# Rounded two-part products for three sums of squares, and one stretch for the scan's small transposes and products

## The chip, the cores and the metric

The kernel runs on one core of one Trainium2 chip. The core has a matrix engine (TensorE, PE in the profile, with its weight loads as PEld), three engines for element work (VectorE or DVE, ScalarE or ACT, GpSimd or POOL) and queues that start transfers (SP's, GpSimd's and ScalarE's). The metric is device time in microseconds (us) of one launch.

## What is computed

The reference is one layer of a streaming encoder for two request groups, 256 prompt positions and 32 sample positions, 288 in all, in float32. Cut to what matters here:

```python
def rmsnorm(x, g):
    y = x * lax.rsqrt(jnp.mean(x * x, axis=-1, keepdims=True) + EPS)
    return y * g

def ssd_scan(xh, dt, A, Bm, Cm, D, h0):          # 32 heads in 2 groups, chunks of 64
    acum = jnp.cumsum(dt * A, axis=-1)            # per chunk
    lmat = jnp.exp(jnp.where(causal, acum[..., :, None] - acum[..., None, :], -jnp.inf))
    cb = jnp.einsum('bclgn,bcsgn->bcgls', Cc, Bc)
    y_diag = jnp.einsum('bcgls,bcgjls,bcsgjp->bclgjp', cb, lmat, xc)
    decay_states = jnp.exp(acum[..., -1:] - acum)
    ...
    return y_diag + y_off + D[..., None] * xh, h_last

def run_layer(x, ...):
    proj = rmsnorm(x, norm_mix_pre) @ w_in        # u, z, xBC, dt
    y_pool = pool_mixer(u, ...)
    y_ssd = ssd_mixer(z, xbc, dt_raw, ...)        # conv, silu, ssd_scan, gate, rmsnorm per group of 1024
    x = x + rmsnorm(concat([y_pool, y_ssd]) @ w_out, norm_mix_post)
    x = x + rmsnorm(ConvFFN(rmsnorm(x, norm_ffn_pre)), norm_ffn_post)
```

## The kernel before

Activations lie with channels on the 128 partitions and the 288 positions along the free axis. Every large product is made of three: weights and activations are each split into a rounded high part and a low part in the format fp32r (`split_w`, L124 to L138; `split_from`, L101), and `mm3` (L141 to L144) adds high times high, high times low and low times high into one accumulator. ScalarE rounds the weights (L136), VectorE subtracts to get the low part (L137), and each pair of tiles comes from a ring of four buffers. `project` (L146) streams the weights from memory through this for 256 output channels at a time.

The stages follow each other: the first stage (`prepare`, the loop over CHUNKS, L324 to L358) multiplies the first 768 columns of w_in while the input arrives, and its order on every engine is written out by hand (`pin`, which puts an instruction behind the one traced before it on its engine). Then come the projections for the scan's channels (xs) and the gates (z), among which eight `ssd_quad` calls do the scan for four heads each; then u and the pooling, w_out, the states, the feed-forward block, and a pinned end. Outside the pinned parts a planner sets the order on each engine from its own estimate of when things are ready and from the order in which the code traced them.

Three places matter.

The sums of squares. A sum over channels is a matmul of a 128x128 tile of float32 ones with a float32 tile of squares, which leaves the sum on every partition. The first is L349, in the next to last chunk of the first stage, behind 24 of its products: ScalarE and VectorE gather the squares in `sq2` (L315 to L318), VectorE adds its two halves (L339), TensorE sums, ScalarE takes the square root (L352), VectorE the reciprocal (L353), and all results of the first stage are scaled by it. `rstd_all` (L659 to L670) does the same for the scan's two groups of 1024 channels (`rg0` in the middle of the z projections, `rg1` after the first u projection; their squares are gathered by GpSimd in `gsum`, L684) and, pinned, for the feed-forward block (`r2`, over `xsum`).

The scan's tables. dt and the running sums g of 32 heads are computed on 32 partitions (L472 to L505). From g come the decay rows `dec` (three exponentials on ScalarE, L510, and one product with dt on VectorE, L511). `ssd_quad` wants them by position, so nine transposes of 32 rows by 128 columns (L518 to L520: g, dt and dec in each of three blocks of positions) go through three PSUM tiles, and VectorE copies each out in two pieces, `tok` and `tokd` (L521, L522).

The head columns and C.B. One 32-row matmul (L530) spreads the skip factor D and the last decay of each head into `dcol`; six matmuls of 128 rows (L546 to L548) make the products of C and B for the two groups, from which VectorE makes the masked table `cbt` (L549 to L552).

Of the kernel before, what the change touches and what calls it, by code (L numbers as in the profile page):

```python
# [16 lines left out]
P = 128  # L17
# [39 lines left out]
def body(  # L57
# [34 lines left out]
    def aux(shape, name):  # L92
        return aux_ps.tile(shape, F32, tag="aux", name=name)
# [230 lines left out]
    for i, (kb, n) in enumerate(CHUNKS):  # L324
# [13 lines left out]
        if i == len(CHUNKS) - 2:  # L338
            pin(dve.tensor_tensor(sq2[:, :NT], sq2[:, :NT], sq2[:, NT:], op=ALU.add))  # L339
        w = ahead_w.pop(0)  # L340
        products = [
# [4 lines left out]
        for q, (r, m, k, x) in enumerate(products):  # L346
            if i == len(CHUNKS) - 2 and q == 24:
                p_ = aux([P, NT], "prs")
                pin(pe.matmul(p_, ones, sq2[:, :NT], start=True, stop=True))  # L349
                rstd = const.tile([P, NT], F32, tag="spread", bufs=3, name="rstd")  # L350
                last_split[:] = [
                    pin(act.activation(rstd, p_, AF.Sqrt, bias=eps_t, scale=1.0 / D_MODEL)),  # L352
                    pin(dve.reciprocal(rstd, rstd)),  # L353
                ]
# [17 lines left out]
    act.activation(g_ssd, col["ssd_norm"], AF.Copy, scale=0.5)  # L372
    sel = const.tile([HEADS, 2], F32, name="sel")
    pick = const.tile([HEADS, NX], F32, name="pick")
    sel64 = const.tile([HEADS, 2, 64], F32, name="sel64")
    with tc.issue_after(last_split[1].ins):
        dve.tensor_reduce(sel, id32.rearrange("h (t r) -> h r t", r=2), axis=AX.X, op=ALU.add)
        dve.tensor_reduce(pick, id32.rearrange("h (t r) -> h t r", r=2), axis=AX.X, op=ALU.add)
        dve.tensor_copy(sel64, sel.unsqueeze(2).broadcast_to([HEADS, 2, 64]))

    start.close()


    mixer = ExitStack()
    mp = mixer.enter_context(tc.tile_pool(name="mixer", bufs=1))
    sc_stage = const.tile([P, 2, 3, NXC], F32, name="sc_stage")
    np_stage = const.tile([P, 2, 15, NU], F32, name="np_stage")
# [107 lines left out]
    dve.tensor_tensor_scan(r, scan_one, adt, 0.0, op0=ALU.mult, op1=ALU.add)  # L495
    g = mp.tile([HEADS, 4, MW], F32, tag="m", bufs=2, name="g")[:, 0, :]
    t0, t1, t2 = r[:, 63:64], r[:, 127:128], r[:, 191:192]
# [9 lines left out]
    sp.dma_start(out=g_d, in_=g)  # L507
    dec = htile("dec", tag="gsum")
    for (o, n), go, last in zip(BLK, (0, 256, 384), (255, 383, 415)):
        act.activation(dec[:, o : o + n], g[:, go : go + n], AF.Exp, bias=g[:, last : last + 1], scale=-1.0)  # L510
    dve.tensor_tensor(dec, dec, dt, op=ALU.mult)  # L511


    tok = mp.tile([P, 3, 2, HEADS], F32, name="tok")
    tokd = const.tile([P, 3, HEADS], F32, name="tokd")
    for b, (o, go) in enumerate(((0, 0), (P, 256), (TAIL, MW - P))):
        p_ = aux([P, 3, HEADS], "ptok")
        pe.transpose(p_[:, 0, :], g[:, go : go + P], id32)  # L518
        pe.transpose(p_[:, 1, :], dt[:, o : o + P], id32)
        pe.transpose(p_[:, 2, :], dec[:, o : o + P], id32)  # L520
        dve.tensor_copy(tok[:, b, :, :], p_[:, 0:2, :])  # L521
        dve.tensor_copy(tokd[:, b, :], p_[:, 2, :])  # L522

# [4 lines left out]
    dve.tensor_scalar(hv[:, NX:], pick, elast, None, op0=ALU.mult)  # L528
    p_ = aux([P, 2 * NX], "phv")
    pe.matmul(p_, sel64.rearrange("h r q -> h (r q)"), hv, start=True, stop=True)  # L530
    dcol = const.tile([P, 2 * NX], F32, name="dcol")
# [11 lines left out]
    for gi in range(2):  # L543
        blocks_out(b_d, gi, bc[gi], mp, 2)
        p_ = aux([P, MW], "pcb")
        pe.matmul(p_[:, 0:256], bc[gi][:, 0:P], bc[2 + gi][:, 0:NP_], start=True, stop=True)  # L546
        pe.matmul(p_[:, 256:384], bc[gi][:, P:NP_], bc[2 + gi][:, P:NP_], start=True, stop=True)
        pe.matmul(p_[:, 384:], bc[gi][:, TAIL:], bc[2 + gi][:, NP_:], start=True, stop=True)  # L548
        dve.tensor_tensor(cbt[:, gi, 0:128], p_[:, 0:128], tri, op=ALU.mult)  # L549
# [108 lines left out]

    def rstd_all(sq, scale, name, pin=False):  # L659

        p_ = aux([P, NT], "psum_t")
        ins = pe.matmul(p_, ones, sq, start=True, stop=True)
        if pin:
            tc.keep_in_program_order(ins)
            sums_at.append(ins)
        with tc.high_priority(offset=800 if pin else 0):
            o = const.tile([P, NT], F32, tag="spread", bufs=3, name=name)
            act.activation(o, p_, AF.Sqrt, bias=eps_t, scale=scale)
            dve.reciprocal(o, o)
        return o  # L670
# [69 lines left out]
    for i in range(NX // 2):  # L740
# [7 lines left out]
        if i == 5:  # L748
            rg.append(rstd_all(gsum[0], 0.25 / 1024, "rg0"))
        run_quads(Z_RATE[i])  # L750
# [19 lines left out]
    ups = [project(win, [(512, 256)], xn, K16)]  # L770
    rg.append(rstd_all(gsum[1], 0.25 / 1024, "rg1"))
    mixer.close()
# [276 lines left out]
    def up(tiles, spare=()):  # L1049
# [5 lines left out]
        def out(m, p_):  # L1055
            waiting.append((each[m], p_))
            if not norm_2 and m == SUMS_AFTER:
                norm_2.append(rstd_all(xsum, 1.0 / D_MODEL, "r2", pin=True))
            while norm_2 and waiting:
# [279 lines left out]
```

## Time and profile before

| | before |
|---|---|
| timed runs, median of 3 | 1336.0 us (1335.72 to 1336.15) |
| profiled execution, first to last instruction (its span) | 1333.3 us |
| granted TensorE clock, mean | 1.000 |
| TensorE busy | 1325.7 us, 99% of the span |
| VectorE, ScalarE, GpSimd busy | 885.5, 665.1, 241.7 us |
| bytes moved by DMA | 249.52 MB |

A profile is one execution, taken by the hardware. Times are from the start of the span. The rows name the line of the kernel, the engine, and out<-in by the program's names. A busy time of a group of matmuls counts overlapping ones once; a single matmul's length includes its way through the array, so the distance from one start to the next, not the length, is what it adds. The chain of waits follows the work that ended last back from the end, and its pieces give that distance; a piece in it stands some 0.07 to 0.17 us later than the start of the same instruction in the timeline. Releasers ("<-") are inferred from semaphores.

### The profile page before, as it was taken

To read this page: it belongs to the slowest core of one execution; us is meant where nothing else is said; L and a number is where in the kernel's file an instruction comes from. 1 tells how busy PE (TensorE), PEld (TensorE's weight loads), DVE (VectorE), ACT (ScalarE), POOL (GpSimd) and SP (SyncE) were. 2 spreads that over 40 slices of the span, in tenths; PEclk is the share of its full clock that TensorE was granted. 3 is DMA by queue.
4 is the path that set the end of the run, shared out by engine and by line. 5 is a ranking of instruction groups with operands and counts; after the bars stand their busy time and mean duration, and the time that the engine had idled before them with its cause. 6 is when DMAs were issued, how large, how long until landed. Compare 5 with 4: busy or idle time off the path is not lost.

```text
span 1333.3 us, 25388 instructions
## 1 busy us (share of the span) xinstructions
PE 1325.7 (99%) x10127; PEld 1314.2 (99%) x10127; DVE 885.5 (66%) x1501; ACT 665.1 (50%) x995; POOL 241.7 (18%) x386
## 2 busy tenths in 40 slices
PE   9999999999999999999999999999999999999998
PEld 9999999999999999999999999999999999999997
DVE  7999987879544488976766643335666666754454
ACT  7557767446443456544444433334454444444442
POOL 2343231222122310211211200001121111201110
PEclk9999999999999999999999999999999999999999
DMA  8678884455555446766554454454554555466753
GB/s 329 192 216 266 272 252 156 155 199 210 190 191 202 143 145 227 210 184 181 167 177 158 153 172 156 160 182 162 179 165 159 167 170 170 159 227 188 206 177 111
DMA packets 110230, 249.52 MB, mean 187 GB/s; under 512 B 64480, under 2 KB 75840, under 8 KB 87584
## 3 DMA queue, kind: packets, MB, share of 16 engines
q1 hardware_dynamic: 105920, 233.61, 54.6%
q0 software_dynamic: 3808, 13.77, 2.9%
q8 instruction: 79, 1.29, 0.4%
q10 hardware_dynamic: 384, 0.52, 0.1%
q14 instruction: 39, 0.32, 0.1%
HBM read 235.91 MB, written 11.95 MB: 186 GB/s over the span
## 4 chain that ended last, share of the span: by engine, by line
PE 98%; DVE 0%; DMA 0%; ACT 0%; SPq 0%; issue 0%
PE acc L142 30%; PE acc L144 30%; PE acc L143 30%; PE acc L355 2%; PE acc_x L355 1%; PE py L613 1%; PE acc L1200 0%; PE acc L1201 0%; DMA xg<-in_x_g 0%; PE acc_t L1223 0%; PE pst L938 0%; PE acc_x L143 0%; PE acc_x L142 0%; PE acc_x L144 0%; PE pst L905 0%; PE py L615 0%
## 5 line engine op out<-in xcount | busy, mean ns | idle before, releaser
L137 DVE TENSOR_TENSOR wlo<-raw,whi 128x1024 fp32r<-128x1024 f32 (+1 forms) x396 | 472.0, 1193 | 346.1 <-ACT whi L136 344.8
L136 ACT ACTIVATE whi<-raw 128x1024 fp32r<-128x1024 f32 (+1 forms) x396 | 408.5, 1033 | 503.2 <-PE acc L143 420.4
L142 PE MATMUL acc<-hn,whi 128*128 128x288 f32 x1376 | 404.3, 296 | 0.0
L143 PE MATMUL acc<-hn,whi 128*128 128x288 f32 x1376 | 403.8, 294 | 0.2 <-DVE hn L994 0.2
L144 PE MATMUL acc<-hn,wlo 128*128 128x288 f32 x1376 | 403.3, 294 | 0.0
L143 PEld LDWEIGHTS acc<-hn,whi 128*128 128x128 f32 x1376 | 259.9, 189 | 0.7 <-DVE hn L994 0.7
L144 PEld LDWEIGHTS acc<-hn,wlo 128*128 128x128 f32 x1376 | 259.9, 189 | 0.0
L142 PEld LDWEIGHTS acc<-hn,whi 128*128 128x128 f32 x1376 | 257.3, 187 | 0.1
L142 PE MATMUL acc<-fa,whi 128*128 128x288 f32 x660 | 195.5, 296 | 0.0
L143 PE MATMUL acc<-fa,whi 128*128 128x288 f32 x660 | 195.4, 296 | 0.0
L144 PE MATMUL acc<-fa,wlo 128*128 128x288 f32 x660 | 195.1, 296 | 0.0
L142 PE MATMUL acc<-xn,whi 128*128 128x288 f32 x608 | 180.8, 297 | 0.0
L143 PE MATMUL acc<-xn,whi 128*128 128x288 f32 x608 | 179.1, 295 | 0.0
L144 PE MATMUL acc<-xn,wlo 128*128 128x288 f32 x608 | 178.8, 294 | 0.0
L143 PEld LDWEIGHTS acc<-fa,whi 128*128 128x128 f32 x660 | 124.5, 189 | 0.0
L142 PEld LDWEIGHTS acc<-fa,whi 128*128 128x128 f32 x660 | 124.1, 188 | 0.0
L144 PEld LDWEIGHTS acc<-fa,wlo 128*128 128x128 f32 x660 | 123.8, 188 | 0.0
L1027 POOL COPY fc_stage<-ebuf 128x4 f32<-128x4 f32 x88 | 25.7, 293 | 503.5 <-DVE ebuf L1026 460.1
L143 PEld LDWEIGHTS acc<-xn,whi 128*128 128x128 f32 x608 | 114.9, 189 | 0.1
L144 PEld LDWEIGHTS acc<-xn,wlo 128*128 128x128 f32 x608 | 114.8, 189 | 0.0
L142 PEld LDWEIGHTS acc<-xn,whi 128*128 128x128 f32 x608 | 114.0, 187 | 0.8 <-issue 0.5
L1033 DVE SCALAR_TENSOR_TENSOR fc<-ebuf,cols,fc 128x290 f32<-128x290 f32 x176 | 90.4, 517 | 2.9 <-ACT fc L1031 0.3
(333 smaller groups left out, 1766.5 us busy)
## 6 DMA issues: line engine op xcount, KB each, us to landing
raw<-in_w_up SPq DMA_DIRECT2D x80, 1024.0 KB, 5.1
raw<-in_w_in SPq DMA_DIRECT2D x38, 1024.0 KB, 5.4
raw<-in_w_down SPq DMA_DIRECT2D x32, 1024.0 KB, 5.0
raw<-in_w_out SPq DMA_DIRECT2D x24, 1024.0 KB, 5.0
raw<-in_w_down SPq DMA_DIRECT2D x16, 768.0 KB, 4.2
raw<-in_w_up SPq DMA_DIRECT2D x14, 512.0 KB, 3.9
gb<-g_d POOLq DMA_DIRECT2D x8, 832.0 KB, 7.1
raw<-in_w_first SPq DMA_DIRECT2D x5, 768.0 KB, 13.0
```

Of the source, the lines that this page charges most:

```text
L136: act.activation(hi, raw[:, k : k + n, :], AF.Copy)
L137: dve.tensor_tensor(lo, raw[:, k : k + n, :], hi.bitcast(F32), op=ALU.subtract)
L142: then(pe.matmul(out, wh, a[:, 0, :], start=start, stop=False))
L143: then(pe.matmul(out, wh, a[:, 1, :], start=False, stop=False))
L144: then(pe.matmul(out, wl, a[:, 0, :], start=False, stop=stop))
L355: pin(pe.matmul(first[m], w[:, k, r * NB + m * P :][:, :P], xn[kb + k][:, x, :], start=kb + k + r + x == 0, stop=kb + k == KD - 1 and r == ...
L613: ins = pe.matmul(y[c, 0:256], xw[:, 0, f_], m[:, h, 0:256], start=True, stop=False)
L1027: pool.tensor_copy(fc_stage[:, :, :, i], e[:, 256:324].rearrange("p (s c) -> p s c", c=34)[:, :, 0:2])
L1033: dve.scalar_tensor_tensor(c, e[:, r_ : r_ + 290], f_w[:, r_, i : i + 1], c, op0=ALU.mult, op1=ALU.add)
```

## The change

The first sum: VectorE makes a rounded copy of the gathered squares and the rest by subtraction, and TensorE adds two fp32r products with a tile of ones that is in fp32r already (`busy`). `rstd_all` does likewise where it isn't pinned, with the rounded copy on ScalarE and a new tile of rounded ones, `ones_r`; the two parts are taken from the mixer's ring "sq" of two buffers. The pinned sum stays.

g, a copy of dt and the decay rows are put on partitions 0 to 31, 32 to 63 and 64 to 95 of one tile, `turned`; the decay product becomes three, one behind each exponential, and two copies bring dt over. Three transposes of 96 rows replace nine, into one PSUM tile that the head columns share, and two copies replace six. `follow` leaves the first of these transposes to the planner and pins each of the rest, the head columns' matmul and the six C.B matmuls behind the one before. `sel`, `pick` and `sel64` move from the constants to the mixer's pool, and `dec` from the ring "gsum" to the ring "z", with 416 columns.

```diff
@@ -337,6 +337,9 @@
             ))
         if i == len(CHUNKS) - 2:
             pin(dve.tensor_tensor(sq2[:, :NT], sq2[:, :NT], sq2[:, NT:], op=ALU.add))
+            sq_r = xin.tile([P, 2 * NT], F32R, tag="sq", bufs=1, name="sq_r")
+            pin(dve.tensor_copy(sq_r[:, :NT], sq2[:, :NT]))
+            pin(dve.tensor_tensor(sq_r[:, NT:], sq2[:, :NT], sq_r[:, :NT].bitcast(F32), op=ALU.subtract))
         w = ahead_w.pop(0)
         products = [
             (r, m, k, x) for m in (2, 3, 4, 5, 0, 1) for k in range(n) for r, x in ((0, 0), (0, 1), (1, 0))
@@ -346,7 +349,8 @@
         for q, (r, m, k, x) in enumerate(products):
             if i == len(CHUNKS) - 2 and q == 24:
                 p_ = aux([P, NT], "prs")
-                pin(pe.matmul(p_, ones, sq2[:, :NT], start=True, stop=True))
+                for c in (slice(0, NT), slice(NT, 2 * NT)):
+                    pin(pe.matmul(p_, busy[:, 0:P], sq_r[:, c], start=c.start == 0, stop=c.start > 0))
                 rstd = const.tile([P, NT], F32, tag="spread", bufs=3, name="rstd")
                 last_split[:] = [
                     pin(act.activation(rstd, p_, AF.Sqrt, bias=eps_t, scale=1.0 / D_MODEL)),
@@ -370,19 +374,20 @@
     act.activation(pah, cols[:, c0 : c0 + 5 * NXC], AF.Copy, scale=0.5)
     g_ssd = const.tile([P, NX], F32, name="g_ssd")
     act.activation(g_ssd, col["ssd_norm"], AF.Copy, scale=0.5)
-    sel = const.tile([HEADS, 2], F32, name="sel")
-    pick = const.tile([HEADS, NX], F32, name="pick")
-    sel64 = const.tile([HEADS, 2, 64], F32, name="sel64")
+    start.close()
+
+
+    mixer = ExitStack()
+    mp = mixer.enter_context(tc.tile_pool(name="mixer", bufs=1))
+    sel = mp.tile([HEADS, 2], F32, name="sel")
+    pick = mp.tile([HEADS, NX], F32, name="pick")
+    sel64 = mp.tile([HEADS, 2, 64], F32, name="sel64")
     with tc.issue_after(last_split[1].ins):
         dve.tensor_reduce(sel, id32.rearrange("h (t r) -> h r t", r=2), axis=AX.X, op=ALU.add)
         dve.tensor_reduce(pick, id32.rearrange("h (t r) -> h t r", r=2), axis=AX.X, op=ALU.add)
         dve.tensor_copy(sel64, sel.unsqueeze(2).broadcast_to([HEADS, 2, 64]))
-
-    start.close()
-
-
-    mixer = ExitStack()
-    mp = mixer.enter_context(tc.tile_pool(name="mixer", bufs=1))
+    ones_r = const.tile([P, P], F32R, name="ones_r")
+    act.activation(ones_r, ones, AF.Copy)
     sc_stage = const.tile([P, 2, 3, NXC], F32, name="sc_stage")
     np_stage = const.tile([P, 2, 15, NU], F32, name="np_stage")
     hist_c = col["hist_c"].rearrange("p (r t) -> p r t", t=NXC)
@@ -493,7 +498,8 @@
     dve.tensor_scalar(adt, dt, aneg, -1.0, op0=ALU.mult, op1=ALU.mult)
     r = htile("r", tag="z")
     dve.tensor_tensor_scan(r, scan_one, adt, 0.0, op0=ALU.mult, op1=ALU.add)
-    g = mp.tile([HEADS, 4, MW], F32, tag="m", bufs=2, name="g")[:, 0, :]
+    turned = mp.tile([P, 4, MW], F32, tag="m", bufs=2, name="g")[: 3 * HEADS, 0, :]
+    g, dt_rows, dec_rows = (turned[HEADS * i : HEADS * (i + 1), :] for i in range(3))
     t0, t1, t2 = r[:, 63:64], r[:, 127:128], r[:, 191:192]
     t12 = htile("t12", 1)
     dve.tensor_tensor(t12, t1, t2, op=ALU.add)
@@ -505,29 +511,34 @@
     dve.tensor_copy(g[:, 320:416], r[:, 192:288])
     g_d = dram.tile([HEADS, MW], F32, name="g_d")
     sp.dma_start(out=g_d, in_=g)
-    dec = htile("dec", tag="gsum")
+    dec = htile("dec", MW, tag="z")
     for (o, n), go, last in zip(BLK, (0, 256, 384), (255, 383, 415)):
-        act.activation(dec[:, o : o + n], g[:, go : go + n], AF.Exp, bias=g[:, last : last + 1], scale=-1.0)
-    dve.tensor_tensor(dec, dec, dt, op=ALU.mult)
-
+        act.activation(dec[:, go : go + n], g[:, go : go + n], AF.Exp, bias=g[:, last : last + 1], scale=-1.0)
+        dve.tensor_tensor(dec_rows[:, go : go + n], dec[:, go : go + n], dt[:, o : o + n], op=ALU.mult)
+    for o, n, go in ((0, P, 0), (P, NT - P, 256)):
+        dve.tensor_copy(dt_rows[:, go : go + n], dt[:, o : o + n])
+
+    small = []
+
+    def follow(ins):
+        return pin(ins) if small else small.append(ins)
 
     tok = mp.tile([P, 3, 2, HEADS], F32, name="tok")
     tokd = const.tile([P, 3, HEADS], F32, name="tokd")
-    for b, (o, go) in enumerate(((0, 0), (P, 256), (TAIL, MW - P))):
-        p_ = aux([P, 3, HEADS], "ptok")
-        pe.transpose(p_[:, 0, :], g[:, go : go + P], id32)
-        pe.transpose(p_[:, 1, :], dt[:, o : o + P], id32)
-        pe.transpose(p_[:, 2, :], dec[:, o : o + P], id32)
-        dve.tensor_copy(tok[:, b, :, :], p_[:, 0:2, :])
-        dve.tensor_copy(tokd[:, b, :], p_[:, 2, :])
+    p_t = aux([P, 9 * HEADS + 2 * NX], "ptok")
+    p_tok = p_t[:, : 9 * HEADS].rearrange("p (b h) -> p b h", b=3)
+    for b, go in enumerate((0, 256, MW - P)):
+        follow(pe.transpose(p_tok[:, b, :], turned[:, go : go + P], ident[: 3 * HEADS, : 3 * HEADS]))
 
     hv = htile("hv", 2 * NX)
     elast = htile("elast", 1)
     act.activation(elast, g[:, 415:416], AF.Exp)
     dve.tensor_scalar(hv[:, 0:NX], pick, hp[:, 2:3], None, op0=ALU.mult)
     dve.tensor_scalar(hv[:, NX:], pick, elast, None, op0=ALU.mult)
-    p_ = aux([P, 2 * NX], "phv")
-    pe.matmul(p_, sel64.rearrange("h r q -> h (r q)"), hv, start=True, stop=True)
+    p_ = p_t[:, 9 * HEADS :]
+    follow(pe.matmul(p_, sel64.rearrange("h r q -> h (r q)"), hv, start=True, stop=True))
+    dve.tensor_copy(tok, p_tok[:, :, : 2 * HEADS].rearrange("p b (r h) -> p b r h", r=2))
+    dve.tensor_copy(tokd, p_tok[:, :, 2 * HEADS :])
     dcol = const.tile([P, 2 * NX], F32, name="dcol")
     dve.tensor_copy(dcol, p_)
 
@@ -543,9 +554,9 @@
     for gi in range(2):
         blocks_out(b_d, gi, bc[gi], mp, 2)
         p_ = aux([P, MW], "pcb")
-        pe.matmul(p_[:, 0:256], bc[gi][:, 0:P], bc[2 + gi][:, 0:NP_], start=True, stop=True)
-        pe.matmul(p_[:, 256:384], bc[gi][:, P:NP_], bc[2 + gi][:, P:NP_], start=True, stop=True)
-        pe.matmul(p_[:, 384:], bc[gi][:, TAIL:], bc[2 + gi][:, NP_:], start=True, stop=True)
+        follow(pe.matmul(p_[:, 0:256], bc[gi][:, 0:P], bc[2 + gi][:, 0:NP_], start=True, stop=True))
+        follow(pe.matmul(p_[:, 256:384], bc[gi][:, P:NP_], bc[2 + gi][:, P:NP_], start=True, stop=True))
+        follow(pe.matmul(p_[:, 384:], bc[gi][:, TAIL:], bc[2 + gi][:, NP_:], start=True, stop=True))
         dve.tensor_tensor(cbt[:, gi, 0:128], p_[:, 0:128], tri, op=ALU.mult)
         dve.tensor_copy(cbt[:, gi, 128:256], p_[:, 128:256])
         dve.tensor_tensor(cbt[:, gi, 256:384], p_[:, 256:384], tri, op=ALU.mult)
@@ -656,13 +667,20 @@
                 tc.keep_in_program_order(ins)
         return p_
 
-    def rstd_all(sq, scale, name, pin=False):
+    def sq_parts(pool_):
+        return [pool_.tile([P, NT], F32R, tag="sq", bufs=2, name="sq_r") for _ in range(2)]
+
+    def rstd_all(sq, scale, name, sq_r, pin=False):
 
         p_ = aux([P, NT], "psum_t")
-        ins = pe.matmul(p_, ones, sq, start=True, stop=True)
         if pin:
-            tc.keep_in_program_order(ins)
+            ins = tc.keep_in_program_order(pe.matmul(p_, ones, sq, start=True, stop=True))
             sums_at.append(ins)
+        else:
+            act.activation(sq_r[0], sq, AF.Copy)
+            dve.tensor_tensor(sq_r[1], sq, sq_r[0].bitcast(F32), op=ALU.subtract)
+            for i in range(2):
+                pe.matmul(p_, ones_r, sq_r[i], start=i == 0, stop=i == 1)
         with tc.high_priority(offset=800 if pin else 0):
             o = const.tile([P, NT], F32, tag="spread", bufs=3, name=name)
             act.activation(o, p_, AF.Sqrt, bias=eps_t, scale=scale)
@@ -746,7 +764,7 @@
         if i == 0:
             xs_conv(NX // 2 - 1)
         if i == 5:
-            rg.append(rstd_all(gsum[0], 0.25 / 1024, "rg0"))
+            rg.append(rstd_all(gsum[0], 0.25 / 1024, "rg0", sq_parts(mp)))
         run_quads(Z_RATE[i])
         for j in range(2):
             gate_silu(2 * i + j)
@@ -768,7 +786,7 @@
 
 
     ups = [project(win, [(512, 256)], xn, K16)]
-    rg.append(rstd_all(gsum[1], 0.25 / 1024, "rg1"))
+    rg.append(rstd_all(gsum[1], 0.25 / 1024, "rg1", sq_parts(mp)))
     mixer.close()
     outp = ExitStack()
     op_ = outp.enter_context(tc.tile_pool(name="outp", bufs=1))
@@ -1055,7 +1073,7 @@
         def out(m, p_):
             waiting.append((each[m], p_))
             if not norm_2 and m == SUMS_AFTER:
-                norm_2.append(rstd_all(xsum, 1.0 / D_MODEL, "r2", pin=True))
+                norm_2.append(rstd_all(xsum, 1.0 / D_MODEL, "r2", None, pin=True))
             while norm_2 and waiting:
                 (kind, j), p_ = waiting.pop(0)
                 conv_[kind, j] = fconv(kind * NF + j, p_)
```

## The prediction

> **What bounds the kernel now.** I read first the head of the profile's page and the summary of the chain that ended last, then the list of waits, longest first.
>
> ```profile
> span 1333.3 us, 25388 instructions
> ...
> PE 1325.7 (99%) x10127; PEld 1314.2 (99%) x10127; DVE 885.5 (66%) x1501; ACT 665.1 (50%) x995; POOL 241.7 (18%) x386
> ...
> PE 98%; DVE 0%; DMA 0%; ACT 0%; SPq 0%; issue 0%
> ```
>
> ```profile
> ACT whi L136 <- PE acc L143: 420.4, 248, 2.8
> DVE wlo L137 <- ACT whi L136: 344.8, 225, 3.2
> ```
>
> TensorE is busy for 99% of the span and makes 98% of the chain. The two waits say the same from the other side: ScalarE, which rounds the weights, waits 420.4 us in all for buffers that TensorE must give back, and VectorE waits for ScalarE. Weights run ahead of the matmuls. So an edit is worth what it changes on TensorE's own queue: the time that its instructions hold the array, and any time for which that queue stands still. A microsecond on another engine counts only where a TensorE instruction then waits for it.
>
> The profiled execution's span is 1333.3 us and the median of the timed runs 1336.0, so 2.7 us lie around the span. The change touches nothing there; I sum against the span and add 2.7 at the end.
>
> **The three sums of squares.** The chain of waits, cut to short windows, gives what each instruction adds to TensorE's chain (start, time, what). The first sum, the group 0 sum and the group 1 sum, with neighbours:
>
> ```profile
> 37.90 0.93 PE acc L355 x7
> 38.84 0.48 PE prs L349 x2
> ```
>
> ```profile
> 242.00 0.49 PE psum_t L662 x2
> ```
>
> ```profile
> 284.61 0.13 PE acc L144
> 284.74 0.49 PE psum_t L662 x2
> 285.22 0.13 PE acc L142
> ```
>
> A float32 sum of 128x288 is one matmul in the code and two in the records (x2); the three hold TensorE for 0.48 + 0.49 + 0.49 = 1.46 us. A rounded product of the same 288 columns takes 0.93 / 7 = 0.133. Each sum becomes two of these: 3 x 2 x 0.133 = 0.80. That is **0.66 us less**, and since both prices stand side by side, the bounds are close to it (0.60 to 0.70). The pinned sum over xsum keeps its form and gives nothing.
>
> Each of the three now needs a rounded copy and a subtraction first. For groups 0 and 1 these are one operation on ScalarE and one on VectorE. What covers them, for group 1: the last addition into gsum, and the first use of the result.
>
> ```profile
> 276.69 1.42 POOL L684 TENSOR_TENSOR gsum<-gsum,sq 128x288 f32<-128x288 f32 x1 [1.49 <-ACT sq L683]
> ```
>
> ```profile
> L821 DVE TENSOR_TENSOR xs<-xs,rg x8: 444/450/452, 291.7 to 321.2; 128x288 f32<-128x288 f32 x8
> ...
> L669 DVE RECIPROCAL rg<-rg x2: 1952/1952/1952, 244.9 to 287.6; 128x288 f32<-128x288 f32 x2
> ```
>
> The sum's input is complete at 276.69 + 1.42 = 278.1, and TensorE takes the sum up at 284.7. Two operations of about 0.46 us (the VectorE row L339 below has that shape) fit into these 6.6 us: nothing on TensorE. If the planner moved the sum later by their 0.9 us, the result would be late by as much; the reciprocal now ends at 287.6 + 1.95 = 289.6, and its first use is at 291.7, so 2.1 us are left. Without the cover it would cost the 0.9. The two parts take both buffers of the ring from which the squares of the gates come, so ScalarE's next square waits for the sum; behind it on ScalarE stand roundings of weights, which have the 420.4 us of waiting to spare.
>
> The first sum has much less cover, and here the change adds a wait to a pinned queue. Its timeline on VectorE and GpSimd, and a row that shows how fast a released product starts:
>
> ```profile
> 37.47 0.46 DVE L339 TENSOR_TENSOR sq<-sq 128x288 f32<-128x288 f32 x1
> ```
>
> ```profile
> 44.73 0.20 POOL L408 COPY sc_stage<-ebuf 128x6 f32<-128x6 f32 x1 [12.78 <-DVE ebuf L402]
> ```
>
> ```profile
> 10.62 0.96 DVE L298 TENSOR_TENSOR w<-raw,w 128x768 fp32r<-128x768 f32 x1 [0.21 <-ACT w L294]
> ```
>
> ```profile
> 11.63 0.53 PE L355 MATMUL acc<-xn,w 128*128 128x288 f32 x2 [0.33 <-DVE w L298]
> ```
>
> The squares are added up by 37.47 + 0.46 = 37.93. For the rounded copy of 288 columns on VectorE the trace holds two neighbours that differ widely:
>
> ```profile
> L305 DVE CAST w<-raw 128x256 fp32r<-128x256 f32 x1 | 1.7, 1669 | 2.6 <-DMA raw<-in_w_first 2.6
> L483 DVE TENSOR_SCALAR ser<-s 32x288 f32<-32x288 f32 x1 | 0.3, 293 | 0.0
> ```
>
> ```profile
> 4.01 1.36 POOL L333 MEMSET ubuf<- 128x350 f32 x4
> ```
>
> The first is the same operation, 1.67 us from 3.86 on, and it ended at 5.53, soon after GpSimd had finished its fills at 4.01 + 1.36 = 5.37. The second is another operation with one input, 0.29 us. GpSimd is idle for the 12.78 us before 44.73, so around 37.9 nothing of it runs, and I take 0.29. [...]
>
> Then the high part is ready at 38.22 and the low part at 38.22 + 0.46 = 38.68. A product started 11.63 - 11.58 = 0.05 us after VectorE released it. In the matmuls' own times the sum starts some 0.17 us before the chain's 38.84, at 38.67, and its second product is due at 38.67 + 0.13 = 38.80. 38.73 against 38.80: no wait, with almost no margin. With the long copy it would be 37.93 + 1.67 + 0.46 + 0.05 = 40.11, a stall of 1.3 us for the products queued behind. On VectorE the next pinned instruction is the reciprocal, which needs the sum's result anyway.
>
> **The transposes, the head columns and C.B.** The chain around the three groups of transposes (the last two lines are from a window of their own):
>
> ```profile
> 99.94 0.17 PE ptok L518
> 100.11 0.06 PE ptok L519
> 100.17 0.33 PE acc L142
> ...
> 100.64 0.17 PE ptok L518
> 100.81 0.06 PE ptok L519
> 100.87 0.06 PE ptok L518
> 100.93 0.06 PE ptok L519
> 101.00 0.33 PE acc L144
> ```
>
> ```profile
> 106.88 0.30 PE ptok L520 x3
> 107.17 0.33 PE acc L142
> ```
>
> A 32-row transpose in a run takes 0.06, but the first of each group costs 0.17 and the product after it 0.33 instead of 0.13. Group by group, less the 0.13 that the product costs anyway: 0.17 + 0.06 + 0.20 = 0.43; 0.17 + 3 x 0.06 + 0.20 = 0.55; 0.30 + 0.20 = 0.50. Together **1.48 us removed**.
>
> In their place come three transposes of 96 rows and 96 columns. No row has that shape. From below: the 32-column 0.06 each, 0.18. From above: 128 columns, from the C.B rows,
>
> ```profile
> 110.41 0.33 PE phv L530 x2
> 110.74 0.63 PE pcb L546 x2
> 111.37 0.22 PE pcb L547 x2
> ...
> 112.61 0.21 PE acc L144
> ```
>
> where two records of 128 columns add 0.22, so 0.11 each, 0.33 for three; and with the entry and exit of a 32-row group (0.11 + 0.20) once more, 0.64. The full-height float32 sums pay no such entry or exit (0.13 follows 0.49), and 96 rows are more than any of the narrow shapes, so I take three quarters of 0.11 each, 0.25. That leaves **1.23 us less** (0.84 to 1.30). [...]
>
> The head columns and C.B products stay as many and as long. Their 32-row matmul still pays for entering and leaving its shape, now between transposes and C.B rather than between a product and C.B: nothing, within 0.1.
>
> What moves is when the stretch can begin. All three tables must now stand in one tile, so the first transpose waits for the decay rows:
>
> ```profile
> 99.62 0.38 ACT L510 ACTIVATE dec<-g 32x128 f32<-32x128 f32 x1
> ```
>
> ```profile
> 100.73 1.20 DVE L137 TENSOR_TENSOR wlo<-raw,whi 128x1024 fp32r<-128x1024 f32 x1
> ...
> 102.29 0.44 DVE L511 TENSOR_TENSOR dec<-dec,dt 32x288 f32<-32x288 f32 x1
> ...
> 103.91 1.23 DVE L137 TENSOR_TENSOR wlo<-raw,whi 128x1024 fp32r<-128x1024 f32 x1 [0.75 <-ACT whi L136]
> ```
>
> The one product L511 becomes three shorter ones and two copies, about 0.2 to 0.3 us each; six copies out of PSUM become two. On VectorE the sum is about level, at most 0.5 us more. The old decay transposes ran at 106.88 although their rows stood at 102.73: the planner keeps 4 us of distance between VectorE's work and TensorE's, and I expect the new stretch at 104 to 107 without a wait. If it did wait, products queue behind it and nothing else on TensorE can pass. The order inside the stretch is one of issue only, so other products may stand between its members; that would cost a fresh entry and exit only around the 32-row one (0.3).
>
> The rest costs nothing: the rounding of the ones is one ScalarE instruction among 665.1 us of work in 1333.3; sel, pick and sel64 change their pool, and their only users are the head columns, 60 us later; no DMA is added or moved on SP's or GpSimd's queue. Sum: -0.66 - 1.23 = -1.89. Span 1331.4, **time 1334.1 us**, 0.14% less. Its own range, with the bounds above, is 1334.0 to 1334.6, and 0.5 wider on either side for what a new plan of the order shifts.
>
> **The rivals.**
>
> *The stretch is held by VectorE.* Place: TensorE's queue at 104 us. If the planner puts the stretch together when the first columns are ready, and the decay rows of the last block come a round of VectorE's work later, TensorE stands. A round is one weight subtraction to the next, 103.91 - 100.73 = 3.2 us. One round gives 1334.1 + 3.2 = 1337.3, two give 1340.5. It eats the gain from 1.9 us on, and shows as slower by over 0.2% from 4.6 us on. For it: VectorE is busy nearly without a break there, and five instructions in place of one are five chances to fall behind a subtraction. Against it: the 4 us of distance, and the weights' waits, which say that VectorE can fall behind for a while unseen. Chance 0.17, 0.10 of it past 1338.7.
>
> *The first sum comes late,* with the long copy: 1334.1 + 1.3 = 1335.4. For it the only row of the very operation; against it the idle GpSimd. Chance 0.08.
>
> *The change does less than it says:* 96 rows pay entry and exit and other products split the stretch, 1334.1 + 0.4 + 0.3 = 1334.8. It lies next to the forecast. Chance 0.13. [...]
>
> *More than priced.* Were the transposes free, 1334.1 - 0.25 = 1333.9; and a new plan might close the one gap in the middle,
>
> ```profile
> 519.79 0.40 PE acc L143
> ```
>
> where a product adds 0.40 instead of 0.13: 1333.6. Past 1333.3 (0.2%) nothing in the profile leads; only luck in the plan or in the measurement. Chance 0.14.
>
> **How the numbers follow.** The forecast has the rest, 0.48. About 0.2% (2.7 us, 1333.3 to 1338.7) is what a measurement of this kernel tells from no change. Faster by over 0.2%: the far half of the last rival and a little of the forecast's spread, 0.13. Slower: the two rounds, 0.10. Within: 0.77. The range leaves out the two-round stall and the far tail of the last rival: 1332.8 to 1337.3.
>
> **What would show it.** In the changed profile: each of the three sums as two records of 0.13 in the chain, none before its parts; three transposes of 96x96 at 0.06 to 0.11 each in one place after 102.7; no entry or exit cost but around the head columns; TensorE still 98% of the chain. An idle line of TensorE released by VectorE near 38.7 or 104 would show the first or second rival. I am wrong if the span falls by less than 1 us without such a line, or by more than 2.6.

## The result and the profile after

| | before | after |
|---|---|---|
| timed runs of one series, median of 21 each | 1335.72 us (1334.36 to 1336.2) | 1333.45 us (1332.8 to 1334.61) |
| ratio, with its 95% interval | | 0.9984 (0.9978 to 0.999) |
| span of the profiled execution | 1333.3 us | 1332.2 us |

The change makes the kernel 2.1 us faster (1.3 to 2.9): within 0.2% of before, as forecast, and close to the 1.9 us of the sum. The spans differ by 1.1 only, for a reason that lies in the start and is told below.

The head of the page and the list of waits of the kernel after:

```profile
span 1332.2 us, 25388 instructions
...
PE 1325.0 (99%) x10121; PEld 1315.0 (99%) x10121; DVE 888.3 (67%) x1505; ACT 665.0 (50%) x998; POOL 246.4 (18%) x386
...
PE 99%; DVE 0%; DMA 0%; ACT 0%; issue 0%
```

```profile
ACT whi L136 <- PE acc L143: 418.7, 247, 2.6
DVE wlo L137 <- ACT whi L136: 335.2, 220, 3.2
```

The bound is the same, and so is the lead of the weights: 418.7 us of ScalarE waiting for TensorE where there were 420.4.

The chain of waits in short windows, around the first sum, the two group sums, the transposes, and the product behind the C.B matmuls (start, time, what):

```profile
38.97 0.53 PE acc L359 x4
39.50 0.27 PE prs L353 x2
```

```profile
241.34 0.26 PE psum_t L683 x2
```

```profile
283.88 0.26 PE psum_t L683 x2
```

```profile
107.70 0.13 PE acc L143
107.83 0.25 PE ptok L531 x3
108.09 0.33 PE ptok L539 x2
```

```profile
110.29 0.21 PE acc L144
```

Each sum now holds TensorE for 0.27, 0.26 and 0.26 us where it held it for 0.48 to 0.49: 0.67 less. The three 96-row transposes take 0.25 together and the product ahead of them its plain 0.13: no entry is paid. The head columns' 0.33 and the 0.21 behind C.B are what they were. So 1.48 became 0.25: 1.23 less. Together 1.90, against 1.89 in the prediction.

The timeline of VectorE before the first sum, and of TensorE there:

```profile
37.58 0.46 DVE L339 TENSOR_TENSOR sq<-sq 128x288 f32<-128x288 f32 x1
38.08 0.31 DVE L341 CAST sq_r<-sq 128x288 fp32r<-128x288 f32 x1
38.42 0.46 DVE L342 TENSOR_TENSOR sq_r<-sq,sq_r 128x288 fp32r<-128x288 f32 x1
```

```profile
39.34 0.43 PE L353 MATMUL prs<-sq_r,busy 128*128 128x288 f32 x2
```

The copy took 0.31 us and the low part was ready at 38.88, before TensorE began the sum at 39.34. The decay rows and the copies of dt come in pieces on VectorE, the last of the decay products here:

```profile
104.07 0.28 DVE L517 TENSOR_TENSOR g<-dec,dt 32x128 f32<-32x128 f32 x1
```

It ends at 104.35, and the stretch starts at 107.7 without a wait: 3.3 us of distance.

**Where the spans' other half microsecond is.** The same stretch of the start, first before, then after:

```profile
5.67 0.77 PE L355 MATMUL acc<-xn,w 128*128 128x288 f32 x4 [0.65 <-DVE w L305]
...
6.91 0.69 PE L355 MATMUL acc<-xn,w 128*128 128x288 f32 x4
```

```profile
5.69 1.30 PE L359 MATMUL acc<-xn,w 128*128 128x288 f32 x4 [0.67 <-DVE w L305]
...
7.27 1.16 PE L359 MATMUL acc<-xn,w 128*128 128x288 f32 x4
```

Four products take 0.69 in the one and 1.16 in the other: TensorE ran at half its pace until 9.2 us in the profile of after, and until 5.9 in that of before, though the granted clock of both is 1.00 in these stretches. The first product of a projection and the last product of the kernel stand at, before and then after:

```profile
47.72 0.40 PE L142 MATMUL acc<-xn,whi 128*128 128x288 f32 x1
```

```profile
1327.82 1.12 PE L1265 MATMUL py__15288<-ft,diag 128*128 128x512 f32 x2 [0.67 <-ACT diag L1264]
```

```profile
48.17 0.40 PE L142 MATMUL acc<-xn,whi 128*128 128x288 f32 x1
```

```profile
1326.71 1.13 PE L1283 MATMUL py__15295<-ft,diag 128*128 128x512 f32 x2 [0.67 <-ACT diag L1282]
```

The first stage ended 0.45 us later than before, in spite of a sum that is 0.22 shorter. From there to the last product it is 1280.10 us before and 1278.54 after: 1.56 less, where two sums and the transposes should give 0.45 + 1.23 = 1.68. The start differs from one profile to the next (the last group of experiments), so I compare the profiles of the experiments by this distance, which I call the body. Each body is that of a single execution; between kernels with the same edits it agrees to 0.15 us, except for e10 (below). It leaves out the first sum, which lies ahead of it.

### The profile page after: what moved, and what is told of

Same layout as the page of the kernel before. It is cut to its first block, busy times and chain, and to the rows that moved or that the text cites. A ratio compares the mean times of both kernels' runs of the same rounds, so it can differ in the third digit from the quotient of the medians.

```text
span 1332.2 us, 25388 instructions
## 1 busy us (share of the span) xinstructions
PE 1325.0 (99%) x10121; PEld 1315.0 (99%) x10121; DVE 888.3 (67%) x1505; ACT 665.0 (50%) x998; POOL 246.4 (18%) x386
## 4 chain that ended last, share of the span: by engine, by line
PE 99%; DVE 0%; DMA 0%; ACT 0%; issue 0%
PE acc L142 30%; PE acc L144 30%; PE acc L143 30%; PE acc L359 2%; PE acc_x L359 1%; PE py L624 1%; PE acc L1218 0%; PE acc L1219 0%; PE acc_t L1241 0%; PE pst L956 0%; PE acc_x L143 0%; PE acc_x L142 0%; PE acc_x L144 0%; PE pst L923 0%; PE py L626 0%; DMA raw<-in_w_first 0%
## 5 line engine op out<-in xcount | busy, mean ns | idle before, releaser
L136 ACT ACTIVATE whi<-raw 128x1024 fp32r<-128x1024 f32 (+1 forms) x396 | 408.2, 1032 | 492.6 <-PE acc L143 418.7
```

The lines of the kernel that those rows point to most:

```text
L136: act.activation(hi, raw[:, k : k + n, :], AF.Copy)
```

## The experiments

Theory: each edit is worth the time for which its matmuls hold TensorE, as long as no TensorE instruction waits. Rivals: the gain comes from one part alone, from the pinned order, or from luck in the plan or the start; and VectorE's side work is not free.

| kernel | median us | ratio to before of the same series (95%) | span | body | against before |
|---|---|---|---|---|---|
| before | 1335.7 | | 1333.3 | 1280.10 | |
| the change | 1333.5 | 0.9984 (0.9978 to 0.999) | 1332.2 | 1278.54 | -1.56 |
| e1, sums alone | 1335.1 | 0.9999 (0.999 to 1.0008) | 1333.9 | 1279.71 | -0.39 |
| e2, stretch alone | 1334.7 | 0.9993 (0.9984 to 1.0002) | 1333.0 | 1278.86 | -1.24 |
| e4, nine narrow transposes | 1335.1 | 1.0 (0.9991 to 1.0009) | 1333.0 | 1279.77 | -0.33 |
| e3, no pins | 1334.1 | 0.999 (0.9981 to 0.9999) | 1332.6 | 1278.52 | -1.58 |
| e5, GpSimd busy | 1334.0, one run | | 1332.3 | 1278.51 | -1.59 |
| e11, fills under way | 1333.2, one run | | 1331.5 | 1278.52 | -1.58 |
| e6, sum late | 1340.3 | 1.0038 (1.0024 to 1.0052) | 1341.0 | 1286.35 | +6.25 |
| e7, 6 us on VectorE | 1333.6 | 0.9986 (0.9977 to 0.9995) | 1331.4 | 1278.64 | -1.46 |
| e8, two more edits | 1332.6 | 0.9978 (0.997 to 0.9987) | 1331.7 | 1277.97 | -2.13 |
| e9, the change, 18 fill matmuls | 1332.9 | 0.9977 (0.9968 to 0.9986) | 1331.4 | 1278.51 | -1.59 |
| e10, e8 with 24 fill matmuls | 1332.7 | 0.998 (0.9971 to 0.9989) | 1332.6 | 1279.15 | -0.95 |
| e12, e8 with 18 fill matmuls | 1333.1 | 0.9982 (0.9973 to 0.9991) | 1331.0 | 1277.82 | -2.28 |

### The two halves

e1 is the kernel before with the first sum's two lines and the new `rstd_all`; e2 is the kernel after with both undone.

```diff
 e2
-            pin(dve.tensor_copy(sq_r[:, :NT], sq2[:, :NT]))
-            pin(dve.tensor_tensor(sq_r[:, NT:], sq2[:, :NT], sq_r[:, :NT].bitcast(F32), op=ALU.subtract))
...
-                    pin(pe.matmul(p_, busy[:, 0:P], sq_r[:, c], start=c.start == 0, stop=c.start > 0))
+                pin(pe.matmul(p_, ones, sq2[:, :NT], start=True, stop=True))
...
-                pe.matmul(p_, ones_r, sq_r[i], start=i == 0, stop=i == 1)
+        ins = pe.matmul(p_, ones, sq, start=True, stop=True)
```

> Only the three sums are changed; nine narrow transposes as before. Theory (each edit is worth the time that its matmuls hold TensorE): each sum adds 0.26 to 0.27 us to TensorE's chain in place of 0.48 to 0.49, together 0.66 us less; the time falls by 0.7 us, ratio to before 0.9995. The nine transposes still cost 1.4 to 1.6 us in three or so groups. Rival (the gain of the whole change comes from the new tables alone): no change in the time, or slower by up to 1.3 us if the first sum's copy comes late.

> Only the tables' transposes and the pinned stretch are changed; all sums stay float32. Theory: three transposes of 96 rows add 0.25 us where nine added 1.48, so the time falls by 1.2 us, ratio 0.9991, and the sums still add 0.48 to 0.49 each. With the run of the sums alone the two add up to the whole change. Rival (the parts hang together by the planner's order): the two gains do not add up to the whole, by more than 0.5 us on TensorE's queue after the first stage.

Neither time alone is told apart from before: runs of one kernel lie up to 2 us apart. The bodies do it: e1 gives 0.39 us, where the two group sums should give 0.45 (the first sum lies ahead of the body), and e2 gives 1.24, as expected. 0.39 + 1.24 = 1.63 against 1.56 for both: the halves add up within 0.1. In e1's chain a group sum is

```profile
243.09 0.26 PE psum_t L677 x2
```

as in the whole change, and in e2 the stretch reads like that of the whole change, the head columns included:

```profile
108.31 0.25 PE ptok L525 x3
108.56 0.33 PE ptok L533 x2
```

### Wide or together: nine narrow transposes in one stretch

```diff
-    for b, go in enumerate((0, 256, MW - P)):
-        follow(pe.transpose(p_tok[:, b, :], turned[:, go : go + P], ident[: 3 * HEADS, : 3 * HEADS]))
+    for b, (o, go) in reversed(list(enumerate(((0, 0), (P, 256), (TAIL, MW - P))))):
+        for i, src in ((2, dec[:, go : go + P]), (0, g[:, go : go + P]), (1, dt[:, o : o + P])):
+            follow(pe.transpose(p_tok[:, b, HEADS * i : HEADS * (i + 1)], src, id32))
```

The shared tile and the copies of dt go as well (not shown), and the blocks come in reverse order.

> The whole change, but with nine transposes of 32 rows in the one pinned stretch in place of three of 96; the first stays free, the rest is pinned behind it. Theory A (the cost is entry and exit of a narrow shape, paid by each group): nine times 0.06 plus one entry of 0.09 to 0.11, since the exit is shared with the 32-row head columns: 0.65 us where the three groups cost 1.48 and the three wide ones 0.25; 0.4 us slower than the whole change. Theory B (the cost is the number of transposes): about 1.2 to 1.5 us for the nine, some 1.0 to 1.2 us slower than the whole change.

1.23 us slower than the whole change by the body, which looks like theory B but isn't. The planner put the nine in two groups, six at 104 us and three at 106.4 in front of the head columns, with thirteen products between them, since a pin fixes order and not neighbourhood:

```profile
103.99 0.24 PE L529 MATMUL ptok<-ident,dec 32*128 32x32 f32 x1
104.07 0.22 PE L529 MATMUL ptok<-ident,g 32*128 32x32 f32 x1
104.13 0.22 PE L529 MATMUL ptok<-ident,dt 32*128 32x32 f32 x1
...
106.39 0.24 PE L529 MATMUL ptok<-ident,dec 32*128 32x32 f32 x1
```

Inside a group they follow each other by 0.06 to 0.08 as theory A has it, and the transposes with the products beside them take 0.6 us more than in the whole change: about the 0.4 of theory A and a second entry and exit of some 0.3. The other 0.6 is a wait elsewhere, in the chain:

```profile
148.90 1.23 DVE wlo L137
150.13 0.04 issue
150.17 0.40 PE acc L144
```

A weight part came late, and 0.74 us lie between two products (149.43 to 150.17) instead of 0.13. The profiled execution (1334.7 us) is the shortest of its ten, so this loss isn't one of a single slow execution. I put it down to the plan, and it comes back below. A single group of nine narrow transposes was not seen, so theory A's 0.65 us for it stays an estimate.

### Without the pins

```diff
     def follow(ins):
-        return pin(ins) if small else small.append(ins)
+        return ins
```

> The whole change without the pins of the stretch: the planner places the three transposes, the head columns and the C.B products freely. Theory (the wide shape does the work, the pins only spare the 32-row matmul an entry and exit of its own): 0 to 0.3 us more on TensorE's queue than the whole change. Rival (the one stretch is what gains): the groups fall apart as before and most of the 1.2 us is lost.

```profile
108.30 0.25 PE ptok L529 x3
108.55 0.33 PE ptok L537 x2
```

The same pieces one behind the other, and the same body to 0.02 us. The planner keeps the stretch together by itself, and the pins are worth nothing that shows here. What gains is three wide transposes that become ready at one moment. How much of that is the shape and how much the smaller number of groups isn't told apart: three narrow groups (before) cost 1.23 us more than the wide transposes, two narrow groups (e4) 0.6.

### Is it GpSimd that makes a rounded copy long?

In the first try (e5) only GpSimd's copy, from 36.82 to 37.51, was under way when the rounded copy started; the fills began at 37.56. The second (e11) has the fills under way.

```diff
+        if i == len(CHUNKS) - 3:
+            pin(pool.tensor_copy(ubuf[0][:, 15:271], sq2[:, NT : NT + 256]))
+            for d in range(20):
+                pin(pool.memset(ubuf[d % 4][:, 15:271], 0.0))
```

> The whole change with one copy of 256 columns and eight fills on GpSimd, started when the squares are complete (near 37.6 us), over columns that are written again later. Theory (the long 1.67 us row of the rounded copy was GpSimd in the way): the copy, 0.31 us in the changed kernel's profile, takes as long as GpSimd works, 1.5 to 2.5 us, and the first sum's products come later by what lies past their due time, about 1 to 2 us of idle TensorE. Rival (the long row was the landing of its input or the first use): the copy stays at 0.31 us and nothing moves.

> The whole change with one copy and twenty fills on GpSimd that start with the squares before the last (near 34 us) and so are under way when the rounded copy starts; the columns are written again later. Theory (a fill in progress holds the copy up, as the long row of 1.67 us suggested): the copy takes over 1 us, ending with the fills near 39 to 40 us, and the first sum waits for it. Rival (the long row had another cause): the copy stays within 0.31 to 0.40 us.

The rounded copy in e5, then the fills and the rounded copy in e11:

```profile
37.28 0.39 DVE L344 CAST sq_r<-sq 128x288 fp32r<-128x288 f32 x1
```

```profile
34.66 5.29 POOL L341 MEMSET ubuf<- 128x256 f32 x20
```

```profile
37.77 0.40 DVE L345 CAST sq_r<-sq 128x288 fp32r<-128x288 f32 x1
```

Twenty fills from 34.66 to 39.95 cost the copy 0.09 us (0.40 for 0.31), and GpSimd's copy in e5 cost it 0.08. What the rivals forecast for the copy (0.31, and 0.31 to 0.40) is about what came. So fills of this kind don't explain the 1.67 us row, and my reason for taking the short price was wrong though the price was right. What made that row long stays open.

### The first sum's input late by 2.1 us

```diff
+            for d in range(6):
+                pin(dve.tensor_tensor(ubuf[d % 4][:, 15:271], sq2[:, :256], sq2[:, NT : NT + 256], op=ALU.add))
             pin(dve.tensor_copy(sq_r[:, :NT], sq2[:, :NT]))
```

The additions go to columns that are written again later.

> The whole change with six VectorE additions of 256 columns (about 0.35 us each, 2.1 us together) ahead of the rounded copy. Theory (the first sum is a wait in TensorE's own queue, with next to no margin): the first sum starts 1.5 to 2.1 us late, TensorE idles for that long before it, and the span grows by it, 1.5 to 2.1 us. Rival (the queue has work enough to cover): under 0.3 us.

Both were wrong. At the sum itself 0.4 us were lost (first main product at 49.20; at 48.77 in e1, whose start was as slow), since TensorE had started slowly and was late too. But the plan behind it became another one, and the profiled execution lost 7.8 us against the whole change in the body. It was the slowest of four (1342.7 us); the others lie at 1339.8 to 1340.4, and by the medians the loss is 6.9 us. The largest piece of it, on VectorE and TensorE:

```profile
190.87 0.96 DVE L605 TENSOR_TENSOR xk<-xk,tok 128x768 f32<-128x768 f32 x1 [1.27 <-DMA xk<-xs_d]
191.74 0.47 DVE L179 STREAM_TRANSPOSE blocks<-xs 128x288 f32<-128x288 f32 x1
192.14 0.42 DVE L722 TENSOR_TENSOR xs<-xs,z 128x288 f32<-128x288 f32 x1
192.47 1.89 DVE L614 TENSOR_TENSOR m<-m,cbt 128x1664 f32<-128x1664 f32 x1
194.27 1.22 DVE L137 TENSOR_TENSOR wlo<-raw,whi 128x1024 fp32r<-128x1024 f32 x1
```

```profile
192.01 0.29 PE L143 MATMUL acc<-xn,whi 128*128 128x288 f32 x1
195.55 0.61 PE L144 MATMUL acc<-xn,wlo 128*128 128x288 f32 x1 [3.24 <-DVE wlo L137]
195.95 0.44 PE L142 MATMUL acc<-xn,whi 128*128 128x288 f32 x1
196.19 0.44 PE L143 MATMUL acc<-xn,whi 128*128 128x288 f32 x1
```

VectorE waits for a transfer of the scan's tokens (1.27 us here; 8.8 us over three such waits between 100 and 200 us, against one of 3.2 in the whole change), uses them, does three more operations, and only then the weight part, whose rounded half ScalarE had finished at 190.63. TensorE idles 3.24 us, and then its products start 0.24 us apart until 201.7, 6 us at half pace; the mean granted clock is 0.87 from 180 to 200 us and 1.00 in the 20 us before. How much of the new plan the six additions caused by their time and how much by chance isn't told apart.

### Six microseconds more on VectorE

```diff
     dec = htile("dec", MW, tag="z")
+    for _ in range(12):
+        dve.tensor_tensor(junk, g, g, op=ALU.add)
```

> The whole change with twelve VectorE additions (32 x 416, about 0.5 us each, 6 us together) on the running sums, traced ahead of the decay rows; their result isn't used. Theory (VectorE runs ahead of TensorE and the planner keeps its distance): the stretch moves later by some us, no idle time of TensorE after the first stage, time as the whole change within 0.3 us. Rival (VectorE is full there): weight parts come late and TensorE idles, 1 to 6 us slower.

```profile
103.08 0.57 DVE L517 TENSOR_TENSOR g<-g 32x416 f32<-32x416 f32 x1
103.69 0.28 DVE L520 TENSOR_TENSOR g<-dec,dt 32x128 f32<-32x128 f32 x1
...
107.65 0.57 DVE L517 TENSOR_TENSOR g<-g 32x416 f32<-32x416 f32 x1
```

The body is that of the whole change to 0.1 us, and the time is its as well within 0.2. But the planner didn't keep the additions together: one ran ahead of the last decay product, a second at 105.58, and the other ten from 107.65 us on. So 6 us more on VectorE, spread out like this, cost nothing. A stretch that is held by VectorE was not tested by this.

In this profile TensorE had started fast, and its first sum shows how small the margin is:

```profile
38.01 0.46 DVE L342 TENSOR_TENSOR sq_r<-sq,sq_r 128x288 fp32r<-128x288 f32 x1
```

```profile
38.33 0.59 PE L353 MATMUL prs<-sq_r,busy 128*128 128x288 f32 x2
```

The two products take from 38.33 to the next product at 38.76, 0.43 instead of 0.27. The low part was ready at 38.47, the second product was due at 38.46 and started at 38.52 (its end at 38.92 less 0.40, the length of the late product at 150.17 in e4), and after this short wait it held TensorE for 0.24 instead of 0.13. In e11, an early start by its first main product (47.52; 47.32 in e7), the low part was ready at 38.66 only, and the reciprocal, which needs the sum's result, started at 39.69 instead of 39.50.

### Two more edits of the kind

```diff
-    follow(pe.matmul(p_, sel64.rearrange("h r q -> h (r q)"), hv, start=True, stop=True))
+    follow(pe.matmul(p_, sel_all.rearrange("h r q -> h (r q)"), hv_all, start=True, stop=True))
...
-                pe.matmul(p_m, ones, msum, start=True, stop=False)
+                act.activation(parts[0], msum, AF.Copy)
+                dve.tensor_tensor(parts[1], msum, parts[0].bitcast(F32), op=ALU.subtract)
+                for i in range(2):
+                    pe.matmul(p_m, ones_r, parts[i], start=i == 0, stop=False)
```

> The whole change, and two edits of the same kind: the head columns' matmul with 96 rows (the upper 64 are zeros) in place of 32, and the sum over msum as two rounded products. Theory: the narrow entry and exits around the head columns go, 0.25 us less, and the sum gives 0.22 us, so 0.45 us less on TensorE's queue than the whole change, ratio to before 0.9980. Rival: the added rounding of msum holds TensorE at its place and eats the gain.

```profile
107.95 0.25 PE ptok L535 x3
108.20 0.17 PE ptok L543 x2
108.37 0.51 PE pcb L561 x2
```

```profile
460.74 0.27 PE psum_m L982 x2
```

The head columns take 0.17 and the first C.B pair 0.51, where they took 0.33 and 0.63 before and in the whole change; the sum takes 0.27 for 0.48. 0.57 less in the body than the whole change, 0.45 expected. The kernel's 1332.6 is the lowest median of all, 0.9978 of before; from the whole change (0.9984 in another series) the times don't tell it apart, the body does.

### The start

e9, e10 and e12 change only `BUSY = 14`, the number of fill matmuls in front of the first product, to 18, 24 (with e8) and 18 (with e8).

> The whole change with 18 instead of 14 fill matmuls in front of the first product, 0.24 us each, so that they reach the first product at 5.7 us without the 0.85 us of idle time. In the profiles so far TensorE's products come down from 0.24 to 0.13 us apart either at 5.9 us (three profiles) or between 9.2 and 10.6 us (seven), and the first main product starts at 47.3 to 47.7 or at 48.2 to 49.2. Theory (unbroken work decides when it speeds up): the early case in every run, the time 0.6 us below that of the whole change and its spread halved. Rival (the moment is chance): the same spread, 1332.8 to 1334.6, and no change of the median.

> The kernel with the head columns on 96 rows and the rounded sum over msum, and 24 fill matmuls, so that TensorE works without a break to 7.0 us. Theory (unbroken work decides): fast from about 6 us in every run, the first main product at 47.7, and the time 0.5 us below the same kernel with 14. Rival (chance): no gain in the median; the first product is late by 1.3 us, which the wait for input near 11 us may hide or not.

> The head columns on 96 rows and the rounded sum over msum, with 18 fill matmuls in front of the first product. Theory (the two edits and the unbroken start add up): TensorE speeds up at 7.3 us as it did with 18 fills, the runs lie within 0.3 us of each other, and the median is 0.4 to 0.5 us below the 1332.86 of the whole change with 18 fills: 1332.4, ratio to before 0.9974. Rival (the moment is chance and the even runs were luck): a spread of 1.5 us as with 14 fills and a median near 1332.6.

e9 seemed to settle it: eleven runs within 0.3 us (1332.81 to 1333.11), 0.6 below the change. e12 took that back: with the same 18 its runs spread from 1332.16 to 1334.2 around 1333.1, and in its profile TensorE speeds up (its starts come down from 0.24 to 0.13 us apart) at 5.1 us, where e9's did at 7.3. e10 sped up at 7.2 and its median is that of e8 (1332.7 and 1332.6), so nothing was gained. All three profiles with 18 or 24 fills sped up by 7.3 us; of the eleven with 14, three did so at 5.9 and seven only between 9.2 and 10.6, and e11 counts with the early ones by its first main product alone (47.52). Unbroken work may thus rule out the late case, which three profiles can't show; within the early ones the moment still varies, and why e9's runs were so even stays open.

e10's 1.2 us of loss against e8 in the body is in part a matter of two weight parts that came late: TensorE waited 0.5 us for them, 0.4 of it for one. But the profiled execution, 1334.3 us, was the slowest of eleven, and the other ten lie between 1332.3 and 1333.1. So most of this loss seems to belong to that execution and not to the plan, which all eleven share.

## Why the prediction was right

**The bound.** TensorE's queue: confirmed by the sum of the pieces (1.90 us by the chain; 1.56 in the body plus the first sum's 0.22 makes 1.78; 2.1 by time, 1.3 to 2.9). The 0.12 us between the first two stay unexplained.

**The sums.** 0.66 forecast, 0.67 measured. The first sum's part of it is in part luck. The margin of 0.07 us was worked out for a fast start, and the profile after had a slow one: TensorE came to the second product 0.59 us after the low part was ready. With a fast start (e7) the second product was 0.06 us late and the sum took 0.43, so that 0.05 of the 0.22 us was left. Whether every fast start loses this isn't shown.

**The transposes.** 1.23 forecast, 1.23 measured; 0.25 for the three wide ones. Here the price was a choice between bounds (0.18 and 0.64), and the argument that 96 rows behave like the full height was the step that held; that three quarters of 0.11 hit the size to 0.01 is luck within these bounds. One is 0.25 us long and adds 0.08.

**The wait added in front of the stretch.** "at 104 to 107 without a wait": 107.7, without a wait. The rival of a stretch held by VectorE didn't occur; no run here provokes it, since in e7 only two of the twelve additions ran ahead of the stretch.

**What was wrong in it.** Four steps. The step "2.7 us lie around the span" set a median beside the span of one launch. In the profiled launches since then 1.7 us lie around it (1333.9 for a span of 1332.2), so that launch took about 1335.0, one of the shorter ones of its kernel (1334.36 to 1336.2). The forecast itself stands, since 1336.0 - 1.89 is the same 1334.1, but not the span of 1331.4: it came out at 1332.2 with a launch that started slowly. The span thus fell by only 1.1 us, close to the 1 us under which the prediction called itself wrong. The margin of the first sum left out what a late product costs beyond its wait, and was gone with a fast start. The reason for the short price of the copy, an idle GpSimd, was wrong (e11), so that the right price was luck. And "a microsecond on another engine counts only where a TensorE instruction then waits for it" is right but was used too lightly: I priced a new plan of the order at 0.5 us. In e4 a wait that I put down to it cost 0.6, and e6 lost about 7 by the medians, some of it perhaps by its additions themselves. That rival, a weight part behind a VectorE instruction that waits for a transfer, was not among mine; in the change as it is the plan happened to be a good one.

## What to carry to other kernels

On a matrix engine that is 99% busy, price an edit by the distance from one start to the next in the chain, not by an instruction's length (0.08 against 0.25 us for a wide transpose), and look for entries and exits of narrow shapes: three groups of small transposes cost six times their replacement (1.48 us against 0.25), one group in a shape of nearly full height. Before pinning a group, see whether the planner keeps it together anyway. And where a planner sets the order, read after each edit who is late next in each engine's queue: a small edit (e6) was followed by a larger loss elsewhere than where it was made. Compare the profiled execution with the other runs of its kernel before its waits are put down to the plan.

## What the hardware showed unexpectedly

A transpose of 32 rows pays 0.11 us on entering from full height (0.17 for 0.06) and the product behind it 0.20; one of 96 rows paid nothing on entering (0.13 ahead of it, 0.25 for three). A product that starts after a short wait holds TensorE for 0.24 us instead of 0.13 (e7; in e4, after a wait of 0.45, from 150.17 to 150.41). TensorE's pace in the first 10 us is half (0.24 us from one start to the next instead of 0.13) until a moment between 5.1 and 10.6 us; the granted clock reads 1.00 meanwhile in the profiles of before and after. With early speed-up (5.1 to 7.3 us) the first main product starts at 47.3 to 48.0, with late at 48.2 to 49.2; how much of the 1.8 us between the runs of one kernel comes from this isn't shown. After 3.24 us of idling in the middle TensorE fell to half pace for 6 us; there the profile does show it, in a mean granted clock of 0.87 from 180 to 200 us (e6).
